# A Hymba decoder layer on one core: the mixer's weights split ahead and kept in DRAM, and work moved between the engines

## The chip, the cores and the metric

One Trainium2 chip, and of it one core. The metric is the device time of one execution in microseconds (us). TensorE is called PE here, VectorE DVE, ScalarE ACT, GpSimd POOL; SyncE (SP) issues all of the kernel's DMAs through one queue, in order.

## The reference

A decoder layer with three sub-layers on 512 tokens of width 1024, in fp32, each modulated from a vector `c` and followed by a layer norm:

```python
h = swiglu_ffn(modulate(x, sh1, sc1), w1, w3, w2)          # D_FF = 2816
x = layer_norm(alpha * x + 0.5 * g1 * h)
h = hybrid_mixer(modulate(x, sh2, sc2), ...)
x = layer_norm(alpha * x + g2 * h)
h = swiglu_ffn(modulate(x, sh3, sc3), ...)
x = layer_norm(alpha * x + 0.5 * g3 * h)

# hybrid_mixer: one input projection, then two groups
# A, 8 heads: indexer scores, the top 128 causal keys of each query, softmax attention over them
# B, 4 heads: short convolution, gated delta rule
proj  = u @ w_in
lower = beta * (k @ k.T) * dec_strict                      # delta rule, per chunk
w, u  = triangular_solve(lower + I, ...)                   # forward substitution
out   = qd @ S + aqk @ delta
dn    = rms_norm(dn, dn_norm_g) * silu(z)
return concat([attn_out, dn]) @ w_out
```

The modulation vectors (`mod`) are `silu(c)` times nine 1024x1024 matrices, 72 blocks of 128x1024 (`wada`).

## The kernel before

Every product of an activation with a weight is made of three matmuls in fp32r: both operands are split into a high part (a rounded copy) and a low part (the rest), and hi x hi, hi x lo and lo x hi are added in PSUM (`mm3`). For a weight block, a load puts 128x1024 into one of five buffers (`raw`), ACT copies 512 columns at a time to `wh`, and DVE or POOL subtracts to `wl` (`weights`; with `pool=True` some of the subtractions are POOL's).

The stages, by the span of the profile: the first gate columns of FFN1 with the first modulation vectors (0 to 62 us); FFN1's loop over 18 blocks of the hidden width (`f`, 48 matmuls of 512 columns each, to 258 us); FFN1's second product, eight output blocks (`dt`, 66 matmuls of 512 columns each) with the layer norm's sums (to 381 us); the norm and the mixer's first six column blocks (tile `g`, weights `wina`, to 421 us); the mixer proper (to about 680 us); its output product and the second norm (to 756 us); FFN2.

The mixer makes 20 projections (`project`, tile `pj`, weights `winb`, 24 matmuls of 512 columns each), the index scores (`ix`), the top-k by repeated maximum on DVE (`m`, `sc`), the softmax (`lg`, `x`; `nm` and `sum` are its row statistics), the values (`pt`, `pth`, `ptl`, `pv`), and the delta rule: `norms` and `pre` (decays `lam`, `er`; products `F`, `aq`), `sub` (forward substitution on 32x32 blocks, tiles `bl` and `Y`, 31 pairs of a multiplication and a subtraction on 64 partitions; its result goes through DRAM to get the layouts `X` and `XT`), `m` (blocks joined to 64 and 128), `rec` (recurrence over four chunks) and `out` (normalisation).

No operation is issued as written. `Graph.add` records all of them, a planner puts them in order by priorities that follow the order of the program, and one line (L561) emits them; rows are therefore read by their tiles. The order of the mixer's parts comes from the string `ORDER`: names with, after a colon, a delay of priority. Buffers are limited: five of `raw`, 86 of 128x512, eight PSUM banks. The modulation blocks (`ada`) are spread over FFN1: two per `f`, three per `dt`.

Of the kernel before, what the change touches and what calls it, by code (L numbers as in the profile page):

```python
# [11 lines left out]
F32 = mybir.dt.float32  # L12
# [15 lines left out]
SKEW, DEFER = 3, 500  # L28
ALPHA = 2.0 ** 0.25
# [535 lines left out]
class Build:  # L565
# [124 lines left out]

    def glu(s, p1, p3):
# [6 lines left out]
    def first_group(s, src, us, halves, big=False):  # L698


        nb = src.shape[2] // P
# [23 lines left out]
    def ffn(s, n, us, halves, ada_plan, res):  # L725
# [11 lines left out]
        for f in range(NF - G0[n]):  # L737
# [7 lines left out]
            s.ada_some(ada_plan(f))  # L745
        ws = {}
        for dt, c0, c1 in pieces(2):
# [11 lines left out]
            s.ada_some(ada_plan(100 + dt))  # L759
# [83 lines left out]
def body(s):  # L843
# [32 lines left out]
    s.ffn(1, us1, ALL, lambda f: 2 if f < 100 else 3, res1)  # L876
# [99 lines left out]
    s.ffn(2, u3, HALF, lambda f: 0, res3)  # L976
# [194 lines left out]
def attend_weights(s, q, k, bias, qt):  # L1171
    nc = s.nc
    w = (qt + 1) * P
    ps = []
    for h in range(4):
# [5 lines left out]
        mx, nm, sm = s.sm(1, "mx"), s.sm(1, "nm"), s.sm(1, "sum")  # L1181
        nc.vector.tensor_tensor_reduce(x[:, :w], pb[:, :w], bias[:, :w], 1.0, GONE, ALU.add, ALU.max, mx)
        nc.vector.tensor_scalar(nm, mx, -0.125, None, op0=ALU.mult)
        nc.scalar.activation(x[:, :w], x[:, :w], AF.Exp, bias=nm, scale=0.125, accum_out=sm)
        nc.vector.reciprocal(sm, sm)
        nc.gpsimd.tensor_scalar(x[:, :w], x[:, :w], sm, 1.0, op0=ALU.mult, op1=ALU.mult)
        ps.append(x)
    return ps


def attend_values(s, ps, v2, qt, g, att):
# [18 lines left out]
    for j in range(2):  # L1210
# [6 lines left out]
ORDER = ("first qi0 qa0:5766 ks:51 pk1:451 spill:57 pk3:1103 pq1:8 z2 qi1:17 gt:131 ix1 pv2:684 pq2:3860 pk2:1987 "  # L1217
# [22 lines left out]
class Mixer:  # L1240
# [59 lines left out]
    def gt(s):  # L1300
# [14 lines left out]
        nc.vector.tensor_copy(s.slr, b.c_("sl"))  # L1315
        cum = b.bank("cum")
# [84 lines left out]
    def pre(s, c):  # L1401
# [38 lines left out]
    def sub(s):  # L1440

        b, nc = s.b, s.nc
        B, n = 32, 64
        bl, Y = (b.g.tile(b.wraw, [P, B * B], F32, "raw", b.name(t), NRAW)[:n] for t in ("bl", "Y"))
        tmp = b.sc[:n]
# [4 lines left out]
        sq3 = lambda x: x.rearrange("p (a b) -> p a b", a=B)  # L1450
# [11 lines left out]
        nc.vector.tensor_copy(sq3(bl), y3.rearrange("p a b -> p b a"))  # L1462
        for src, lst, nme, eng in ((Y, s.X, "dX", nc.vector), (bl, s.XT, "dXT", nc.gpsimd)):
            d = b.g.tile(b.dram, [n, B * B], F32, nme, nme)
            nc.sync.dma_start(d, src)
            g = b.t("G").rearrange("p (u j) -> p u j", u=16)
            nc.sync.dma_start(g, d.rearrange("(u b) (i j) -> (b i) u j", u=16, i=B))
            for c in range(4):
                lst[c] = b.t("X")
                eng.tensor_mul(lst[c].rearrange("p (h b j) -> p h b j", h=4, b=4),  # L1470
                               g[:, 4 * c:4 * c + 4].unsqueeze(2).broadcast_to([P, 4, 4, B]),
                               b.c_("blk").unsqueeze(1).unsqueeze(3).broadcast_to([P, 4, 4, B]))

    def m(s, m, c):

        b, nc, hs, X, XT = s.b, s.nc, s.hs, s.X[c], s.XT[c]
        lm = b.t("lm")
        nc.gpsimd.tensor_mul(h4(lm), h4(s.F[c]), bc4(b.c_(f"m{m}")))
        p1 = b.bank("y1")
        for h in range(4):  # L1480
            nc.tensor.matmul(p1[:, hs[h]], lm[:, hs[h]], X[:, hs[h]], start=True, stop=True)
        y1 = b.t("y1")
        nc.scalar.activation(y1, p1, AF.Copy)
        p3 = b.bank("y3")
        for h in range(4):
            nc.tensor.matmul(p3[:, hs[h]], y1[:, hs[h]], XT[:, hs[h]], start=True, stop=True)
        if m < 128:
            p2 = b.bank("y2")
            for h in range(4):
                nc.tensor.matmul(p2[:, hs[h]], XT[:, hs[h]], y1[:, hs[h]], start=True, stop=True)  # L1490
            nc.vector.tensor_sub(X, X, p2)
        nc.vector.tensor_sub(XT, XT, p3)
# [46 lines left out]
    def out(s, c):  # L1539
# [74 lines left out]
```

## Time and profile before

| | us |
|---|---|
| median of 3 runs | 1100.04 (1100.03 to 1100.62) |
| profiled execution, its own time | 1099.98 |
| its span | 1098.2 |
| PE busy | 1061.3 |
| DVE busy | 679.3 |
| ACT busy | 414.9 |
| POOL busy | 302.3 |

The profiled execution is read by stages of the span: the table of windows gives, for each, how long every engine was busy, and the clock that PE was granted (1.00 is 2.4 GHz, 0.50 is 1.2 GHz). Some 1.8 us of the execution lie outside the span.

### The profile page before, as it was taken

To read this page: it belongs to the slowest core of one execution; us is meant where nothing else is said; L and a number is where in the kernel's file an instruction comes from. 1 tells how busy PE (TensorE), PEld (TensorE's weight loads), DVE (VectorE), ACT (ScalarE), POOL (GpSimd) and SP (SyncE) were. 2 spreads that over 40 slices of the span, in tenths; PEclk is the share of its full clock that TensorE was granted. 3 is DMA by queue.
4 is the path that set the end of the run, shared out by engine and by line. 5 is a ranking of instruction groups with operands and counts; after the bars stand their busy time and mean duration, and the time that the engine had idled before them with its cause. 6 is when DMAs were issued, how large, how long until landed. Compare 5 with 4: busy or idle time off the path is not lost.

```text
span 1098.2 us, 15160 instructions
## 1 busy us (share of the span) xinstructions
PE 1061.3 (97%) x5520; PEld 904.5 (82%) x5520; DVE 679.3 (62%) x1506; ACT 414.9 (38%) x866; POOL 302.3 (28%) x308
## 2 busy tenths in 40 slices
PE   8999999999999989999969999999999999999996
PEld 6788888888888988787747898989888888888896
DVE  7997655547672466999988999884333323333314
ACT  3353323233231434765832566443333322322203
POOL 4600000000222695496824311695000000002210
PEclk9999999999999999998959999999999999999998
DMA  9878555547642412131112303611323222243002
GB/s 359 314 278 316 206 179 196 172 138 244 221 156 91 137 54 98 40 109 46 44 43 52 103 21 125 235 45 41 113 83 110 92 81 72 68 144 106 16 1 77
DMA packets 52203, 137.92 MB, mean 126 GB/s; under 512 B 11360, under 2 KB 15584, under 8 KB 52128
## 3 DMA queue, kind: packets, MB, share of 16 engines
q1 hardware_dynamic: 52048, 136.69, 37.4%
q8 instruction: 43, 0.70, 0.3%
q14 instruction: 32, 0.26, 0.1%
q0 software_dynamic: 80, 0.26, 0.1%
HBM read 131.17 MB, written 5.77 MB: 125 GB/s over the span
## 4 chain that ended last, share of the span: by engine, by line
PE 75%; DVE 15%; issue 3%; ACT 3%; POOL 3%; DMA 1%; SPq 0%; POOLq 0%; ACTq 0%; DVEq 0%
PE p L561 37%; PE y L561 26%; PE g L561 6%; DVE sc L561 2%; DVE raw L561 2%; POOL wl L561 2%; DVE m L561 1%; PE pv L561 1%; DVE cv L561 1%; DVE x L561 1%; PE pj L561 1%; DVE u L561 1%; DVE Y L561 1%; PE pt L561 1%; DVE ptl L561 1%
## 5 line engine op out<-in xcount | busy, mean ns | idle before, releaser
L561 DVE TENSOR_TENSOR wl<-raw,wh 128x512 fp32r<-128x512 f32 (+1 forms) x260 | 180.1, 709 | 151.8 <-ACT wh L561 79.5
L561 ACT ACTIVATE wh<-raw 128x512 fp32r<-128x512 f32 (+1 forms) x300 | 174.7, 615 | 186.1 <-PE y L561 82.4
L561 PE MATMUL p<-ul,wh 128*128 128x512 f32 x592 | 230.3, 389 | 0.0
L561 PE MATMUL p<-uh,wh 128*128 128x512 f32 x592 | 230.3, 389 | 0.0
L561 PE MATMUL p<-uh,wl 128*128 128x512 f32 x592 | 230.3, 389 | 0.0
L561 PE MATMUL y<-hh,wl 128*128 128x512 f32 (+1 forms) x440 | 152.9, 347 | 0.0
L561 PE MATMUL y<-hl,wh 128*128 128x512 f32 (+1 forms) x440 | 152.7, 347 | 0.0
L561 PE MATMUL y<-hh,wh 128*128 128x512 f32 (+1 forms) x440 | 152.5, 347 | 0.0
L561 DVE CUSTOM_DVE_ANT_0 raw<-raw,silu_c 128x1024 f32<-128x1024 f32 x72 | 96.8, 1354 | 75.5 <-DMA raw<-in_wada_dram 75.5
L561 POOL TENSOR_SCALAR s<-x 128x512 f32<-128x512 f32 x3 | 4.0, 1332 | 461.4 <-DVE x L561 461.4
L561 PEld LDWEIGHTS p<-ul,wh 128*128 128x128 f32 x592 | 111.2, 188 | 23.2
L561 PEld LDWEIGHTS p<-uh,wl 128*128 128x128 f32 x592 | 111.1, 188 | 22.9
L561 PEld LDWEIGHTS p<-uh,wh 128*128 128x128 f32 x592 | 111.2, 188 | 22.8
L561 PEld LDWEIGHTS y<-hh,wh 128*128 128x128 f32 x440 | 83.3, 189 | 10.4
L561 PEld LDWEIGHTS y<-hl,wh 128*128 128x128 f32 x440 | 83.3, 189 | 10.4
L561 PEld LDWEIGHTS y<-hh,wl 128*128 128x128 f32 x440 | 83.3, 189 | 10.2
L561 ACT ACTIVATE hh<-sil 128x512 fp32r<-128x512 f32 x44 | 27.7, 633 | 154.9 <-DVE sil L561 135.0
L561 PE MATMUL g<-ul,wh 128*128 128x256 f32 (+1 forms) x256 | 78.8, 319 | 1.7 <-DVE ul L561 1.6
L561 PE MATMUL g<-uh,wh 128*128 128x256 f32 (+1 forms) x256 | 66.4, 316 | 9.9 <-ACT uh L561 9.9
L561 PE MATMUL g<-uh,wl 128*128 128x256 f32 (+1 forms) x256 | 75.5, 316 | 0.0
L561 POOL TENSOR_TENSOR wl<-wb,wh 128x512 fp32r<-128x512 f32 (+1 forms) x48 | 61.1, 1295 | 22.6 <-DMA wb<-in_f1a_dram 18.1
L561 POOL TENSOR_TENSOR s<-s,x 128x512 f32<-128x512 f32 (+1 forms) x21 | 28.5, 1356 | 137.0 <-DVE x L561 126.0
(254 smaller groups left out, 1826.8 us busy)
## 6 DMA issues: line engine op xcount, KB each, us to landing
raw<-in_wada_dram SPq DMA_DIRECT2D x72, 512.0 KB
raw<-in_f2b_dram SPq DMA_DIRECT2D x38, 512.0 KB
raw<-in_f1b_dram SPq DMA_DIRECT2D x36, 512.0 KB
raw<-in_winb_dram SPq DMA_DIRECT2D x20, 512.0 KB
raw<-in_f1c_dram SPq DMA_DIRECT2D x16, 512.0 KB
raw<-in_f2c_dram SPq DMA_DIRECT2D x16, 512.0 KB
wb<-in_f1a_dram SPq DMA_DIRECT2D x16, 256.0 KB
raw<-in_wout_dram SPq DMA_DIRECT2D x8, 512.0 KB
```

Of the source, the lines that this page charges most:

```text
L561: getattr(getattr(s.nc, o.eng), o.meth)(*[real(x) for x in o.args], **{k: real(v) for k, v in o.kw.items()})
```

## The change

1. `presplit`, called in FFN1 once per `f` and twice per `dt`, takes a weight block of the mixer (8 of `wina`, 128x768; 20 of `winb`, 128x1024), loads it to `raw`, splits it (ACT copies to a second `raw` buffer, DVE subtracts in place) and writes both halves to DRAM. In the mixer `stored` loads hi and lo; nothing is split there any more for these 28 blocks.
2. The `ada` blocks are three per `dt` only for the first four `dt`; the last eight move to FFN2.
3. `sub` runs on 128 partitions: the even columns of `Y` on the lower 64, the odd on the upper. One transposed copy (`YT`) goes through DRAM instead of two; `X` is made by transposes on PE and an ACT copy.
4. `m`: the parts that are known to be zero are left out; no mask product on POOL for 128.
5. Softmax: `nm` and `sum` are made for four heads in one instruction; the final scaling of `x` goes from POOL to ACT.
6. `pre`: the decay products `lam` and the scaling of `er` go from POOL to ACT, in pieces of one head; the mask becomes one more matmul.
7. `norms`: squares from POOL to ACT. `out`: the Newton steps of `rsqrt` on DVE become one power on POOL; the scaling of `o` goes from DVE to ACT.
8. `ORDER` is another string.

```diff
+PRE_F, PRE_D = 1, 2
+    def presplit(s):
+        nc = s.nc
+        if s.pre_next >= KD + 20:
+            return
+        i, s.pre_next = s.pre_next, s.pre_next + 1
+        n, src = (768, s.d["wina"][i]) if i < KD else (1024, s.d["winb"][i - KD])
+        dst = s.dwa[i] if i < KD else s.dwb[i - KD]
+        raw = s.wload(src, n)
+        hi = s.g.tile(s.wraw, [P, 1024], F32, "raw", s.name("rawh"), NRAW)
+        nc.scalar.activation(hi[:, :n].bitcast(F32R), raw[:, :n], AF.Copy)
+        nc.vector.tensor_sub(raw[:, :n].bitcast(F32R), raw[:, :n], hi[:, :n])
+        nc.sync.dma_start(dst[0], hi[:, :n])
+        nc.sync.dma_start(dst[1], raw[:, :n])
+    def stored(s, src, n, big=False):
...
+                x = s.g.tile(s.wraw, [P, 1024], F32, "raw", s.name("wd"), NRAW)
+                nc.sync.dma_start(x[:, :n], src[j])
...
+    def plan(s, f):
+        s.ada_some(2 if f < 100 else 3 if f < 104 else 0)
+        for _ in range(PRE_F if f < 100 else PRE_D):
+            s.presplit()
...
-        w = s.weights(s.d["winb"][i + b], 1024, pool=True)
+        w = s.stored(s.dwb[i + b], 1024)
...
-        nc.vector.tensor_scalar(nm, mx, -0.125, None, op0=ALU.mult)
-        nc.scalar.activation(x[:, :w], x[:, :w], AF.Exp, bias=nm, scale=0.125, accum_out=sm)
-        nc.vector.reciprocal(sm, sm)
-        nc.gpsimd.tensor_scalar(x[:, :w], x[:, :w], sm, 1.0, op0=ALU.mult, op1=ALU.mult)
+    nc.vector.tensor_scalar(nm, mx, -0.125, None, op0=ALU.mult)
+    for h, x in enumerate(ps):
+        nc.scalar.activation(x[:, :w], x[:, :w], AF.Exp, bias=nm[:, h:h + 1], scale=0.125, accum_out=sm[:, h:h + 1])
+    nc.vector.reciprocal(sm, sm)
+    for h, x in enumerate(ps):
+        nc.scalar.activation(x[:, :w], x[:, :w], AF.Identity, scale=sm[:, h:h + 1])
...
-            nc.gpsimd.tensor_mul(h4(lam), bc4(b.c_("triu")),
-                                 part[:, 4 * c:4 * c + 4].unsqueeze(2).broadcast_to([P, 4, P]))
-            nc.tensor.matmul(eb, s.slr, lam, start=j == 0, stop=j == 1)
+            for h in range(4):
+                i = c * 4 + h
+                nc.scalar.activation(lam[:, hs[h]], b.c_("triu"), AF.Identity, scale=part[:, i:i + 1])
+            nc.tensor.matmul(eb, s.slr, lam, start=j == 0, stop=False)
+        nc.tensor.matmul(h4(eb), s.idr, bc4(s.below), start=False, stop=True)
...
-            t3 = tmp[:, 0:r * (j + 1)].rearrange("p (a b) -> p a b", a=r)
-            nc.vector.tensor_mul(t3, b3[:, j, j + 1:B].unsqueeze(2).broadcast_to([n, r, j + 1]),
-                                 y3[:, j, 0:j + 1].unsqueeze(1).broadcast_to([n, r, j + 1]))
-            nc.vector.tensor_sub(y3[:, j + 1:B, 0:j + 1], y3[:, j + 1:B, 0:j + 1], t3)
+            r, m = B - 1 - j, j // 2 + 1
+            t3 = tmp[:, 0:r * m].rearrange("p (a b) -> p a b", a=r)
+            nc.vector.tensor_mul(t3, b3[:, j, j + 1:B].unsqueeze(2).broadcast_to([P, r, m]),
+                                 y3[:, j, 0:m].unsqueeze(1).broadcast_to([P, r, m]))
+            nc.vector.tensor_sub(y3[:, j + 1:B, 0:m], y3[:, j + 1:B, 0:m], t3)
...
+            px = b.bank("X")
+            for h in range(4):
+                nc.tensor.transpose(px[:, hs[h]], XT[:, hs[h]], b.c_("ident"))
+            X = s.X[c] = b.t("X")
+            nc.scalar.activation(X, px, AF.Copy)
...
-        cf = b.rsqrt(v, 4)
+        cf = b.sm(4, "cf")
+        nc.gpsimd.tensor_tensor(cf, v, b.c_("mhalf").broadcast_to([P, 4]), op=ALU.pow)
         nc.vector.tensor_mul(cf, cf, rq4)
         for h in range(4):
-            nc.vector.tensor_scalar(o[:, hs[h]], o[:, hs[h]], cf[:, h:h + 1], None, op0=ALU.mult)
+            nc.scalar.activation(o[:, hs[h]], o[:, hs[h]], AF.Identity, scale=cf[:, h:h + 1])
```

Three places of the order that comes out of it. The first is SP's queue in FFN1's loop. Before, one `f` issues four loads, two of weights for FFN1 (`in_f1b`) and two of modulation blocks:

```order
L561 DMA raw_777<-in_f1b_dram 128x1024
L561 DMA raw_796<-in_f1b_dram 128x1024
L561 DMA raw_807<-in_wada_dram 128x1024
L561 DMA raw_815<-in_wada_dram 128x1024
L561 DMA raw_826<-in_f1b_dram 128x1024
```

Now one `f` issues seven:

```order
L562 DMA raw_1079<-in_wina_dram 128x768
L562 DMA raw_1087<-in_f1b_dram 128x1024
L562 DMA raw_1103<-in_f1b_dram 128x1024
L562 DMA raw_1107<-in_wada_dram 128x1024
L562 DMA dwa<-rawh_1101 128x768
L562 DMA dwa<-raw_1079 128x768
L562 DMA raw_1143<-in_wada_dram 128x1024
```

What moved: a load of a mixer block stands ahead of FFN1's own, and two writes, which need ACT's and DVE's halves, stand ahead of the second modulation block. Six `raw` buffers are taken per `f` where four were.

The second is DVE at the start of `sub` (`tmp` or `silu_c` takes the product). Before, on 64 partitions, among it the low parts `ptl` of the attention values:

```order
L561 RECIPROCAL sum_5313<-sum_5313 128x1
L561 RECIPROCAL sum_5318<-sum_5318 128x1
L561 TENSOR_TENSOR silu_c<-bl_5075,Y_5277 64x31
L561 TENSOR_TENSOR Y_5277<-Y_5277,silu_c 64x31
L561 TENSOR_TENSOR silu_c<-bl_5075,Y_5277 64x60
L561 TENSOR_TENSOR Y_5277<-Y_5277,silu_c 64x30x2
L561 TENSOR_TENSOR silu_c<-bl_5075,Y_5277 64x87
L561 TENSOR_TENSOR ptl_5336<-pt_5320,pth_5331 128x512
L561 TENSOR_TENSOR Y_5277<-Y_5277,silu_c 64x29x3
```

Now, on 128 partitions, among the last of the top-k:

```order
L562 TENSOR_TENSOR tmp_5355<-bl_5111,Y_4932 128x31
L562 MAX m_932_5357<-sc_4395 128x8
L562 TENSOR_TENSOR Y_4932<-Y_4932,tmp_5355 128x31
L562 MATCH_REPLACE sc_4395<-m_932_5357,sc_4395 128x256
L562 TENSOR_TENSOR tmp_5355<-bl_5111,Y_4932 128x30
L562 TENSOR_SCALAR sc_4395<-sc_4395 128x256
L562 TENSOR_TENSOR Y_4932<-Y_4932,tmp_5355 128x30
L562 TENSOR_TENSOR tmp_5355<-bl_5111,Y_4932 128x58
L562 TENSOR_TENSOR Y_4932<-Y_4932,tmp_5355 128x29x2
```

What moved: the substitution stands beside the last rounds of the top-k instead of beside the attention's values, and its second and third pairs are half as wide.

The third is ACT's queue where the softmax and the values of several heads stand. Before, exponentials (`x,sum<-x,nm`) are followed at once by the high parts `pth` of the transposed weights:

```order
L561 ACTIVATE x_5267,sum_5289<-x_5267,nm_5281 128x384
L561 ACTIVATE x_5270,sum_5299<-x_5270,nm_5293 128x384
L561 ACTIVATE x_5284,sum_5313<-x_5284,nm_5305 128x384
L561 ACTIVATE x_5295,sum_5318<-x_5295,nm_5308 128x384
L561 ACTIVATE pth_5331<-pt_5320 128x512
L561 ACTIVATE pth_5355<-pt_5341 128x512
```

Now the scalings (`x<-x,sum`), the copies of `X` and the exponentials of the next heads stand in one queue:

```order
L562 ACTIVATE x_5716,sum_5763<-x_5716,nm_5731 128x384
L562 ACTIVATE th_5844<-pj_5586 128x512
L562 ACTIVATE x_5722,sum_5852<-x_5722,nm_5773 128x512
L562 ACTIVATE x_5733,sum_5852<-x_5733,nm_5773 128x512
L562 ACTIVATE X_5872<-X_5861 128x512
L562 ACTIVATE ath_5416<-pv_5837 128x128
L562 ACTIVATE ath_5425<-pv_5837 128x128
L562 ACTIVATE x_5688<-x_5688,sum_5763 128x384
L562 ACTIVATE X_5891<-X_5876 128x512
```

What moved: a scaling that POOL made beside ACT now waits its turn behind ACT's other work, and the copy that the delta rule needs stands between exponentials.

## Rows read from the trace of the kernel before

**Rows 1.** Busy time of each engine by stage, PE's granted clock, DMA share, GB/s.
```profile
62.00:258.00 196.00, 196.00 (x867) 162.34 (x866) 125.66 (x239) 63.44 (x116) 0.00 (x0) 1.00 0.61 207
258.00:381.00 123.00, 123.00 (x676) 107.63 (x675) 65.40 (x134) 33.76 (x63) 34.92 (x31) 1.00 0.51 165
381.00:421.00 40.00, 37.13 (x297) 36.74 (x297) 20.66 (x40) 11.49 (x27) 38.85 (x48) 0.96 0.29 104
421.00:500.00 79.00, 77.36 (x350) 62.96 (x349) 74.14 (x172) 54.47 (x119) 47.89 (x40) 0.98 0.21 69
500.00:540.00 40.00, 37.98 (x192) 31.11 (x191) 38.31 (x101) 26.94 (x66) 28.69 (x29) 0.91 0.17 56
540.00:580.00 40.00, 29.78 (x125) 21.29 (x125) 35.37 (x131) 17.77 (x49) 18.10 (x30) 0.70 0.10 30
580.00:620.00 40.00, 38.88 (x216) 32.63 (x215) 34.57 (x64) 11.80 (x22) 13.22 (x11) 1.00 0.33 93
620.00:680.00 60.00, 59.67 (x455) 55.23 (x454) 55.92 (x247) 39.16 (x127) 9.66 (x16) 1.00 0.17 58
```

**Rows 2.** Groups of PE's waits, 381 to 740 us: total us, times, longest.
```profile
PE pv L561 <- ACT pth L561: 4.0, 5, 1.3
PE pt L561 <- POOL x L561: 1.1, 3, 0.7
```

**Rows 3.** PE in order of time, one wait of the attention: start, us, idle before.
```profile
561.48 0.58 PE L561 MATMUL pv<-pth,vh 128*128 128x256 f32 x1 [0.69 <-ACT pth L561]
```

**Rows 4.** Groups of DVE's instructions, 421 to 710 us: busy, mean ns, idle before.
```profile
L561 DVE TENSOR_TENSOR wl<-raw,wh 128x512 fp32r<-128x512 f32 x31 | 28.0, 926 | 4.4 <-ACT wh L561 4.4
...
L561 DVE TENSOR_TENSOR qs<-rp,qs 64x512 fp32r<-64x512 f32 x16 | 14.5, 904 | 0.4
...
L561 DVE TENSOR_TENSOR Y<-Y,silu_c 64x31 f32<-64x31 f32 (+15 forms) x31 | 12.6, 407 | 0.9
L561 DVE TENSOR_TENSOR silu_c<-bl,Y 64x31 f32<-64x31 f32 (+15 forms) x31 | 11.6, 375 | 1.1 <-POOL x L561 0.2
L561 DVE TENSOR_TENSOR X<-X,y 128x512 f32<-128x512 f32 x12 | 7.9, 683 | 1.3 <-PE y L561 1.2
...
L561 DVE RECIPROCAL sum<-sum 128x1 f32<-128x1 f32 x32 | 4.9, 156 | 1.4 <-ACT x L561 1.3
...
L561 DVE TENSOR_SCALAR nm<-mx 128x1 f32<-128x1 f32 x32 | 4.4, 143 | 0.0
...
L561 DVE TENSOR_SCALAR o<-o,rs 128x128 f32<-128x128 f32 x16 | 3.8, 282 | 0.0
...
L561 DVE TENSOR_TENSOR rs<-rs,rs 128x4 f32<-128x4 f32 (+1 forms) x15 | 3.3, 234 | 0.1
```

**Rows 5.** Groups of POOL's instructions, 381 to 710 us.
```profile
L561 POOL TENSOR_TENSOR wl<-raw,wh 128x512 fp32r<-128x512 f32 x36 | 48.4, 1360 | 28.7 <-ACT wh L561 20.8 <-PE pj L561 7.9
L561 POOL TENSOR_SCALAR x<-x,sum 128x256 f32<-128x256 f32 (+3 forms) x32 | 19.1, 605 | 61.7 <-DVE nm L561 30.7 <-PE pt L561 14.9 <-DVE sum L561 10.9
```

**Rows 6.** Groups of ACT's instructions, 381 to 710 us.
```profile
L561 ACT ACTIVATE wh<-raw 128x512 fp32r<-128x512 f32 x65 | 38.5, 628 | 24.3 <-DMA raw<-in_wout_dram 15.7 <-DMA raw<-in_f2b_dram 6.8 <-PE pj L561 1.7
L561 ACT ACTIVATE x<-x,nm 128x256 f32<-128x256 f32 (+3 forms) x32 | 17.7, 556 | 15.6 <-DVE nm L561 13.9 <-issue 1.6
...
L561 ACT ACTIVATE ktok<-ktok,nm 128x128 f32<-128x128 f32 x16 | 5.0, 412 | 0.0
```

**Rows 7.** Groups of DVE's instructions in FFN1's loop, 62 to 258 us.
```profile
L561 DVE TENSOR_TENSOR wl<-raw,wh 128x512 fp32r<-128x512 f32 x79 | 52.4, 680 | 11.5 <-PE p L561 9.9 <-ACT wh L561 1.3
L561 DVE CUSTOM_DVE_ANT_0 raw<-raw,silu_c 128x1024 f32<-128x1024 f32 x40 | 48.6, 1224 | 51.4 <-DMA raw<-in_wada_dram 51.4
```

**Rows 8.** Busy time in the window with the most DMA traffic, columns as in the first group.
```profile
20.00:40.00 20.00, 17.62 (x68) 13.71 (x69) 19.93 (x27) 6.96 (x12) 14.53 (x9) 0.91 1.04 399
```

**Rows 9.** The chain that ended last: a load of 512 KB, start, us.
```profile
598.38 4.51 DMA raw<-in_wout_dram
```

More of the change, by code (lines that the diff above doesn't have):

```diff
@@ L643, in weights, with get @@
         return get
+    def presplit(s):
[12 more added lines that the diff above has]
+    def stored(s, src, n, big=False):
+        nc = s.nc
+        parts = []
+        for j in range(2):
+            if big:
+                ts = []
+                for o in range(0, n, 512):
+                    m = min(512, n - o)
+                    q, s.g.quota = s.g.quota, s.quota
+                    x = s.t("wd")[:, :m]
+                    s.g.quota = q
+                    s.g.late = s.g.ahead
+                    nc.sync.dma_start(x, src[j][:, o:o + m])
+                    s.g.late = 0
+                    ts.append(x)
+                parts.append(ts)
+            else:
+                x = s.g.tile(s.wraw, [P, 1024], F32, "raw", s.name("wd"), NRAW)
+                nc.sync.dma_start(x[:, :n], src[j])
+                parts.append([x[:, o:o + 512] for o in range(0, n, 512)])
+        def get(i):
+            o = (i % 4) * P
+            return tuple(ts[i // 4][:, o:o + P].bitcast(F32R) for ts in parts)
+        return get
     def mm3(s, out, wh, wl, xh, xl, start, stop):
@@ L744, in ffn @@
             hs.append(s.glu(p1, p3))
-            s.ada_some(ada_plan(f))
+            ada_plan(f)
         ws = {}
@@ L758, in ffn @@
                 del ws[dt]
[L759 removed]
+            ada_plan(100 + dt)
     def rsqrt(s, v, w, n=3):
@@ L1174, in attend_weights @@
     ps = []
+    mx, nm, sm = s.sm(4, "mx"), s.sm(4, "nm"), s.sm(4, "sum")
     for h in range(4):
@@ L1315, in gt @@
         nc.vector.tensor_copy(s.slr, b.c_("sl"))
+        s.idr, s.below = b.keep(P, "idr", F32R), b.keep(P, "below", F32R)
+        nc.vector.tensor_copy(s.idr, b.c_("ident"))
+        nc.vector.tensor_scalar(s.below, b.c_("sl"), NEG, None, op0=ALU.mult)
         cum = b.bank("cum")
@@ L1440, in sub @@
     def sub(s):
[L1442 to L1445, printed above, removed]
+        b, nc, hs = s.b, s.nc, s.hs
+        B, n, w = 32, 64, 16
+        bl = b.g.tile(b.wraw, [P, B * B], F32, "raw", b.name("bl"), NRAW)
+        Y, YT, tmp = b.t("Y"), b.t("YT"), b.t("tmp")
         for c in range(4):
@@ L1462, in sub @@
[L1462 to L1472, printed above, removed]
@@ new lines, in sub @@
+        nc.vector.tensor_copy(YT.rearrange("p (a b) -> p a b", a=w), y3.rearrange("p a b -> p b a"))
+        d = b.g.tile(b.dram, [n, B * B], F32, "dXT", "dXT")
+        halves = d.rearrange("b (m q) -> b m q", m=w)
+        for odd in range(2):
+            nc.sync.dma_start(halves[:, :, odd * B:odd * B + B],
+                              YT[odd * n:odd * n + n].rearrange("p (a b) -> p a b", a=w))
+        g = b.t("G").rearrange("p (u j) -> p u j", u=16)
+        nc.sync.dma_start(g, d.rearrange("(u b) (i j) -> (b i) u j", u=16, i=B))
@@ new lines, in sub @@
+        for c in range(4):
+            XT = s.XT[c] = b.t("XT")
+            nc.vector.tensor_mul(XT.rearrange("p (h b j) -> p h b j", h=4, b=4),
+                                 g[:, 4 * c:4 * c + 4].unsqueeze(2).broadcast_to([P, 4, 4, B]),
+                                 b.c_("blk").unsqueeze(1).unsqueeze(3).broadcast_to([P, 4, 4, B]))
+    def m(s, m, c):
+        b, nc, hs, XT = s.b, s.nc, s.hs, s.XT[c]
+        if m == 64:
+            px = b.bank("X")
[3 more added lines that the diff above has]
+            nc.scalar.activation(X, px, AF.Copy)
+            lm = b.t("lm")
+            nc.gpsimd.tensor_mul(h4(lm), h4(s.F[c]), bc4(b.c_("m64")))
+            p1, p2, p3 = b.bank("y1"), b.bank("y2"), b.bank("y3")
+            for h in range(4):
+                nc.tensor.matmul(p1[:, hs[h]], lm[:, hs[h]], X[:, hs[h]], start=True, stop=True)
+            y1 = b.t("y1")
+            nc.scalar.activation(y1, p1, AF.Copy)
+            for h in range(4):
+                nc.tensor.matmul(p3[:, hs[h]], y1[:, hs[h]], XT[:, hs[h]], start=True, stop=True)
+            for h in range(4):
+                nc.tensor.matmul(p2[:, 32 * h:32 * h + 32], XT[:, hs[h]], y1[:, h * P:h * P + 32], start=True, stop=True)
+            x = h4(X)[:, :, 0:32]
+            nc.vector.tensor_sub(x, x, p2[:, 0:P].rearrange("p (h j) -> p h j", h=4))
+            x, y = (v.rearrange("p (u j) -> p u j", u=8)[:, :, 32:64] for v in (XT, p3))
+            nc.vector.tensor_sub(x, x, y)
+            return
+        X, F, a, e = s.X[c], s.F[c], slice(0, 64), slice(64, 128)
+        p1, p3 = b.bank("y1"), b.bank("y3")
@@ L1487, in m @@
[L1487 to L1492, printed above, removed]
+            nc.tensor.matmul(p3[a, 64 * h:64 * h + 64], y1[e, 64 * h:64 * h + 64], XT[e, h * P + 64:h * P + P],
+                             start=True, stop=True)
+        x = h4(XT)[a, :, 64:128]
+        nc.vector.tensor_sub(x, x, p3[a, 0:256].rearrange("p (h j) -> p h j", h=4))
```

47 lines of the change are left out of this document (22 added, 25 removed), and 10 rows, old and new, of the table ORDER.

## The prediction

> **What bounds the kernel now.** I read the table of stages first [rows 1]. In FFN1 the matmul engine is busy all the time at full clock: 867 matmuls in 196.00 us are 0.226 us each, and nothing but fewer or later matmuls could change these stages. From 381 to 680 us it is not. There I add, stage by stage, what PE stands idle (2.9, 1.6, 2.0, 10.2, 1.1, 0.3: 18.2 us) and what it loses to the lower clock, which is the missing share of the clock times the stretch (0.04 x 40, 0.02 x 79, 0.09 x 40, 0.30 x 40: 18.8 us). Together that is 37 us, an upper bound for the loss, since some of the low clock falls on idle time. The stretch from 500 to 580 us has 27.8 of the 37. Second, in the same table, who is full there: DVE is busy 73.7 of those 80 us, and 238.3 of the 259 us from 421 to 680, while PE's work in these 259 us, without idle time and at full clock, would be 259 - 15.3 - 17.2 = 226.5 us. So DVE has more to do than PE in the mixer. Third, the waits: the groups that end PE's idle time are ACT's `pth` and POOL's scaled `x` [rows 2], short links of the attention's chain [rows 3]. I read the two together so: DVE sets the pace of the stretch, and where its queue is late, PE waits on whatever link it feeds.
>
> **What the change takes from DVE in the mixer** [rows 4]. (a) `sub`: 62 instructions of mean 391 ns. A one-column instruction takes 143 to 156 ns, so some 150 is fixed and 240 goes with width; half the columns give 270 ns: 62 x 0.12 = 7.5 us. (b) Row statistics: 64 instructions become 16, of the same 0.15 us: 7.2 us. (c) The scaling of `o`: 3.8 us. (d) Newton steps: four calls of about a dozen narrow instructions, 0.14 to 0.23 us each, 7 to 11 us; I take 8. (e) `m`: 12 subtractions of 683 ns become four each of 128, 256 and 256 columns, some 0.28 and twice 0.42 us by interpolation: 3.5 us. (f) DVE's instructions are longer while POOL works: `wl` takes 926 ns here and 680 in FFN1's loop [rows 4, 7], where POOL does nothing [rows 1]; `qs` takes 904 where `X`, as wide, takes 683. These two groups alone are 7.6 + 3.5 = 11 us, and POOL gives up its largest groups [rows 5]. Sum 41 us: 238 becomes 197, under PE's 226. The new copies (one `YT` for one `bl`, four `XT` for four `X`) cancel.
>
> **What it adds to ACT there** [rows 6]. Out: 40 splits of `winb`, 25 us. In: 32 scalings of `x`, which are as wide as the exponentials (0.556 us): 17.8; 32 `lam`, 16 `er` and 16 `o` pieces of 128 columns with a scale from a column, as `ktok` has (0.412 us): 26.4; squares and copies of `X`, eight of about 0.6: 5. ACT had 150 us in 421 to 680 [rows 1]; it gets 174 of about 229. It remains below PE; the cover is the slack of 55 us, and it is thinnest after `sub`, which is the second rival's place. The row statistics now wait for four heads together, so a first head starts later by up to three DVE instructions; I leave that in what is not recovered.
>
> Here a rule speaks against the change. `ktok` on ACT takes 412 ns, `o` on DVE, as wide, 282 [rows 4, 6]: a multiplication is 0.13 us cheaper on DVE. The Trainium skill ("ScalarE: Activation LUTs", Rules for kernel authors) says that multiplications belong on VectorE and not on ScalarE; the rows agree in direction. By the rule the 64 narrow pieces waste 64 x 0.13 = 8.3 us, and the time would be 1088 rather than 1080 if all of it lay on the path. By the rows only the 16 `o` come from DVE, and DVE is the full engine, so I charge nothing.
>
> **What it adds to FFN1.** 28 blocks are read and written twice over. Compute: in the loop, 18 subtractions on DVE of up to twice 0.68 us are at most 24.5 us beside 125.7 of 196 busy, and 18 copies on ACT about 23 us beside 63.4 [rows 1, 7]; PE covers both. Traffic: the loop moves 207 GB/s x 196 us = 40.6 MB and gets 25.1 MB more, 335 GB/s. That is under the 399 GB/s that the startup reaches [rows 8]. The first four `dt` each move 1.44 MB of own weights, three modulation blocks (1.57 MB) and two presplit blocks (3.15 MB): 6.16 MB, 15.4 us at 399 GB/s against 66 x 0.226 = 14.9 us. That is 0.5 us each, 2 us in all, as a middle: nothing if the weights split ahead cover it, 9 us if the rate is a tenth lower.
>
> Buffers: a loop pass takes six of the five `raw` slots in 10.85 us, so a slot may be held 9.0 us on average. By the rows a load takes 4.5 us from issue to landing [rows 9], two high parts 1.26 [rows 6], two low parts 1.36 or a modulation product 1.22 [rows 7]; a write, which no row shows, I take like the load. That gives 7.1 for a weight slot, 5.7 for a modulation slot, 11.6 for the presplit's first buffer and 5.8 for its second: mean 7.2 us. In the first four `dt` it is 7.3 us against 7.5 allowed. It just fits, so I charge nothing for it here. In the mixer a projection holds two of the five slots for 24 x 0.226 = 5.4 us, and its successor's two loads and the first of the next fit in the other three: no charge.
>
> **PE's own work.** 16 transposes of 128 columns between 0.06 and 0.23 us each (a quarter and the whole of a 512-column matmul) and four mask matmuls of 0.23 come in; narrower matmuls in `m` go out, at most about what the transposes cost. Bounds -1 to +4.5; I take 2.5, nearer the upper end, since the transposes are of fp32 and their rows could be dearer than a quarter.
>
> **The sum.** PE recovers 25 of the 37 us: nine tenths of the 27.8 between 500 and 580, where DVE is full; the remaining 9 us I leave, since part of it is the norm's chain ahead of 421 us, which stays. 25 - 2.5 - 2 = 20.5 us. The profiled execution took 1099.98 us, 1.8 over its span and equal to the median of the runs (1100.04) to within 0.1 us, so the forecast is 1080. Its own range: all 37 recovered and the other terms at their good ends give 1064; half recovered (18) with 4.5 and 3 against it, 1090.
>
> **Rivals.**
> *ACT becomes the bound behind `sub`.* From 620 to 680 us ACT is busy 39.2 of 60 us already [rows 1]; half of the 32 scalings (9), all `o` (6.6) and the copies of `X` (2.4) would make it 57 to 60 us, with the waits of a queue in order on top. If the stretch keeps its length rather than giving way to other work, about 10 us of the gain go: 1090. For it: the scaled `x` and the copy of `X` stand between exponentials. Against it: the new order can take exponentials earlier, into 540 to 620, where ACT was busy 29.6 of 80 us. Chance 0.17. (The Trainium skill's rule on multiplications, "ScalarE: Activation LUTs", Rules for kernel authors, would be paid for here.)
>
> *The attention's chain stays the wait.* The change doesn't do what it seems to: PE waits 0.7 us a time for `pth` [rows 3], a chain of PE, ACT, DVE and PE that is as long as ever, and the link from POOL only changes engine. If the holes around 560 us are such latencies, the low clock stays too, and a few of the 28 us return: 4 + 2 - 2.5 - 2, between 1096 and 1100. Against it: these named waits are only 5.1 us in all [rows 2] beside 18 of idle time. Chance 0.11.
>
> *FFN1 starves (the other side).* Mechanism: a `raw` slot is held longer than reckoned, because SP issues in order and a write that waits for DVE's half keeps the next loads behind it. A pass of the loop then lasts 6/5 of the hold, a `dt` twice the hold. At 2 us more (9.2 and 9.3) this is 18 x 0.2 + 4 x 3.7 = 18 us; at 2.5 us more 18 x 0.8 + 4 x 4.7 = 33 us, and the time is about 1111. It decides from some 2.2 us on, where the gain of 22.5 is gone. For it: the fit is 7.3 of 7.5. Against it: what is split ahead lies between, and the loop has 1.8 us of room. A milder form is the rate: the Trainium skill ("DMA: Bandwidth & Descriptors", Specifications) gives a core about 358 GB/s of HBM; by it a `dt` would last 17.2 us, 9 us in all, and the time be 1087. The startup's 399 GB/s [rows 8] contradict it for reads; no row has writes in such number. Chance that the end is above before: 0.12.
>
> **The numbers.** Forecast 0.60, ACT-bound 0.17, chain stays 0.11, FFN1 starves 0.12. Predicted 1080. The range reaches from 1065 to 1098: it holds nearly all of the first, the second and most of the third, some 0.83. A measurement of this kernel can tell 0.2% (2.2 us) from no change: faster 0.83 (the first two and half of the third), same 0.04, slower 0.13.
>
> **What would show it.** Right: in FFN1 PE stays at 100% and clock 1.00, DMA near 335 GB/s in the loop; in the stretch of the mixer PE's clock is 1.00 nearly throughout, DVE's busy share falls below 90%, the two instructions of `sub` take about 270 ns, `wl` returns to about 680. ACT-bound: the waits of PE after `sub` are all for ACT and ACT is over 95% busy for 40 us. Chain: the low clock is where `pv` waits for `pth`. Starved: PE waits for `wl` or `wh` between 62 and 345 us, and SP's queue waits for `rawh` or the presplit's subtraction.

## The result and the profile after

The changed kernel takes 1085.49 us (median of four runs, 1082.78 to 1086.81) against 1100.03: a ratio of 0.9865 with an interval of 0.9844 to 0.9886. It is faster by 14.5 us, clear of the scatter of both, where 20 were forecast. The profiled execution took 1084.83 us with a span of 1083.1.

The stages after, in the same windows as [rows 1] (busy time of PE, weight loads, DVE, ACT, POOL; PE's clock; DMA share; GB/s):

```profile
62.00:258.00 196.00, 196.00 (x866) 162.38 (x865) 139.22 (x243) 79.97 (x131) 0.00 (x0) 1.00 0.91 324
258.00:381.00 123.00, 117.10 (x602) 100.52 (x602) 72.69 (x124) 37.38 (x63) 21.21 (x19) 0.97 0.78 280
381.00:421.00 40.00, 38.63 (x323) 38.43 (x323) 21.73 (x49) 9.00 (x20) 25.23 (x35) 1.00 0.46 152
421.00:500.00 79.00, 78.10 (x377) 62.91 (x377) 65.33 (x148) 49.49 (x120) 10.06 (x8) 1.00 0.33 119
500.00:540.00 40.00, 39.26 (x210) 32.65 (x209) 39.91 (x115) 28.77 (x74) 8.96 (x11) 1.00 0.37 123
540.00:580.00 40.00, 39.53 (x215) 32.88 (x214) 38.02 (x131) 20.66 (x57) 2.59 (x2) 1.00 0.46 157
580.00:620.00 40.00, 37.90 (x275) 33.57 (x274) 30.45 (x110) 37.23 (x110) 1.02 (x1) 1.00 0.30 86
620.00:680.00 60.00, 60.00 (x402) 53.95 (x401) 52.84 (x130) 42.75 (x115) 14.39 (x10) 1.00 0.42 138
```

From 421 to 680 us PE now has the full clock throughout and 4.2 us of idle time, where it had 15.3 and a clock of 0.70 at worst. But from 258 to 381 us, where it never waited, it has 5.9 us of idle time and a clock of 0.97, and it does 602 matmuls there instead of 676. A new loss stands where there was none.

Windows of equal time hold different work in the two kernels. The next table therefore goes by events: the starts of the first and last matmuls of a stage in each trace (all times in us).

| stage | before | after | change |
|---|---|---|---|
| FFN1's last product | at 380.9 | at 389.7 | +8.8 |
| the mixer's first column blocks (`g`) | 41.0 | 37.9 | -3.1 |
| from there to the last product of `wout` | 292.7 | 269.7 | -23.0 |
| from there to the last `g` of FFN2 | 40.8 | 43.4 | +2.6 |
| rest of FFN2 | 330.3 | 330.0 | -0.3 |

The sum is -15.0 us. What ended PE's longest waits after the change, from 52 to 756 us (total, times, longest):

```profile
PE y L562 <- ACT wh L562: 5.9, 1, 5.9
PE st L562 <- DVE s L562: 2.2, 2, 1.4
PE g L562 <- ACT uh L562: 1.9, 3, 1.4
PE pv L562 <- DVE ptl L562: 1.0, 2, 0.7
...
PE pv L562 <- DVE sum L562: 0.4, 1, 0.4
...
PE pt L562 <- ACT x L562: 0.3, 1, 0.3
```

The attention's waits of [rows 2], 5.1 us, are down to 1.7. The longest wait is now one of 5.9 us for a weight of FFN1. The chain of what ended last, in order of time (start, us), tells how it came about:

```profile
295.43 1.07 ACT rawh L562
296.50 0.02 issue
296.53 1.24 DVE raw L562
297.78 0.44 SPq L562
298.22 0.04 issue
298.29 0.03 issue
298.31 6.22 DMA raw<-in_f1c_dram
...
317.88 1.22 DVE raw L562
319.09 0.02 DVE mod L562
319.13 3.62 DMA raw<-in_f1c_dram
...
322.83 0.64 ACT wh L562
323.47 0.04 issue
323.51 50.01 PE y L562 x275
```

A presplit block is split; only then SP's queue goes on to the load of FFN1's own weights, which takes 6.2 us to land. A second time the load stands until DVE has finished with a modulation block (`mod`) at 319.1, since no slot was free. Between the two, DVE was busy with the rotary tables (`cos`, `sin`). What SP's queue itself waited for from 250 to 345 us (total, times, longest):

```profile
SPq L562 <- ACT rawh L562: 23.4, 6, 6.1
...
SPq L562 <- DVE mod L562: 10.7, 5, 4.5
```

The loss of 8.8 us is more than the wait. PE in order of time (start, us), and the window behind the wait:

```profile
323.51 0.80 PE L562 MATMUL y<-hh,wh 128*128 128x512 f32 x1 [5.90 <-ACT wh L562]
324.10 0.63 PE L562 MATMUL y<-hl,wh 128*128 128x512 f32 x1
324.53 0.63 PE L562 MATMUL y<-hh,wl 128*128 128x512 f32 x1
```
```profile
322.00:332.00 10.00, 8.49 (x26) 6.73 (x27) 5.10 (x8) 5.03 (x9) 3.52 (x3) 0.66 0.83 302
```

The granted clock, 1.00 up to the wait, is at its lower level behind it (0.50 from 323.6 to 328 us): the starts of the next thirteen matmuls are 0.59 us (once) and 0.43 us apart, where they were 0.227 apart before. So 6.1 us of the 8.8 are PE standing and 2.8 are the lower clock.

In the mixer, the engines from the last of its first blocks to the first product of `wout`, before (first row) and after (second):

```profile
422.00:664.40 242.40, 227.13 (x1241) 190.00 (x1239) 222.09 (x632) 141.10 (x352) 115.42 (x119) 0.93 0.20 62
```
```profile
427.60:647.30 219.70, 215.50 (x1253) 181.84 (x1253) 194.52 (x566) 156.89 (x418) 23.89 (x23) 1.00 0.35 119
```

The stage is 22.7 us shorter. PE stands idle in it for 4.2 us instead of 15.3, and it is busy for 215.5 us instead of 227.1 with about as many matmuls (1253 and 1241), while the granted clock is 1.00 instead of 0.93: about half of the gain is idle time, the other half is clock. For this stage DVE has 27.6 us less to do, POOL 91.5 less and ACT 15.8 more. The groups on DVE that answer to [rows 4] (428 to 698 us; busy, mean ns):

```profile
L562 DVE TENSOR_TENSOR wl<-raw,wh 128x512 fp32r<-128x512 f32 x32 | 29.7, 954 | 0.6 <-ACT wh L562 0.5
...
L562 DVE TENSOR_TENSOR qs<-rp,qs 64x512 fp32r<-64x512 f32 x16 | 11.0, 686 | 1.3 <-ACT qs L562 0.9
L562 DVE TENSOR_TENSOR Y<-Y,tmp 128x126 f32<-128x126 f32 (+22 forms) x31 | 7.9, 254 | 0.6
L562 DVE TENSOR_TENSOR tmp<-bl,Y 128x126 f32<-128x126 f32 (+22 forms) x31 | 7.8, 253 | 1.0 <-issue 0.4
...
L562 DVE RECIPROCAL sum<-sum 128x4 f32<-128x4 f32 x8 | 1.4, 172 | 2.6 <-ACT x L562 2.6
L562 DVE TENSOR_SCALAR nm<-mx 128x4 f32<-128x4 f32 x8 | 1.3, 162 | 0.0
```

`sub`'s two groups are 15.7 us instead of 24.2, `qs` is back to 686 ns, and `wl` is not: 954 ns.

### The profile page after: what moved, and what is told of

Same layout as the page of the kernel before. It is cut to its first block, busy times and chain, and to the rows that moved or that the text cites. A ratio compares the mean times of both kernels' runs of the same rounds, so it can differ in the third digit from the quotient of the medians.

```text
span 1083.1 us, 15160 instructions
## 1 busy us (share of the span) xinstructions
PE 1052.2 (97%) x5540; PEld 898.4 (83%) x5540; DVE 677.2 (63%) x1424; ACT 448.5 (41%) x941; POOL 186.9 (17%) x185
## 4 chain that ended last, share of the span: by engine, by line
PE 75%; DVE 12%; DMA 5%; ACT 3%; issue 3%; POOL 1%; SPq 1%; POOLq 0%; ACTq 0%; DVEq 0%
PE p L562 37%; PE y L562 23%; PE g L562 5%; PE pj L562 4%; DVE raw L562 3%; DVE sc L562 2%; DMA raw<-in_f1c_dram 2%; DVE m L562 1%; PE pv L562 1%; DMA raw<-in_winb_dram 1%; DVE x L562 1%; DVE cv L562 1%; DVE u L562 1%; DMA wd<-dwb 1%; ACT rl L562 1%
## 5 line engine op out<-in xcount | busy, mean ns | idle before, releaser
L562 ACT ACTIVATE wh<-raw 128x512 fp32r<-128x512 f32 (+1 forms) x260 | 149.1, 611 | 131.1 <-PE y L562 48.3
L562 DVE CUSTOM_DVE_ANT_0 raw<-raw,silu_c 128x1024 f32<-128x1024 f32 x72 | 100.3, 1399 | 40.0 <-DMA raw<-in_wada_dram 39.8
L562 PE MATMUL pj<-uh,wd 128*128 128x512 f32 x320 | 104.6, 399 | 0.5 <-DMA wd<-dwb 0.4
L562 ACT ACTIVATE rawh<-raw 128x1024 fp32r<-128x1024 f32 (+1 forms) x28 | 28.0, 1000 | 107.2 <-DMA raw<-in_winb_dram 73.6
L562 PEld LDWEIGHTS pj<-uh,wd 128*128 128x128 f32 x320 | 59.4, 188 | 13.8 <-DMA wd<-dwb 1.5
L562 PE MATMUL pj<-ul,wd 128*128 128x512 f32 x160 | 62.3, 395 | 0.0
L562 ACT ACTIVATE hh<-sil 128x512 fp32r<-128x512 f32 x44 | 27.6, 631 | 83.4 <-DVE sil L562 70.9
```

Source lines behind the costliest of these rows:

```text
L562: getattr(getattr(s.nc, o.eng), o.meth)(*[real(x) for x in o.args], **{k: real(v) for k, v in o.kw.items()})
```

## The experiments

Stage times below are read from the profiled execution, by the first and last matmuls as in the table above; "the mixer" is its third row. In three of the kernels the line that emits all operations is L563.

**Why FFN1 is late: slots or bytes.** One more slot:

```diff
-NBIG, NRAW, WF, WM, WB, W2 = 86, 5, 32, 16, 28, 28
+NBIG, NRAW, WF, WM, WB, W2 = 84, 6, 32, 10, 28, 28
```

> The changed kernel with six raw slots instead of five (paid for with two of the 86 small buffers and a smaller quota of split weights in the mixer, so the mixer may lose a little). It asks why FFN1 ends 8.8 us later than before (389.7 instead of 380.9 us). Theory S, slots and order: SP's in-order queue waits for a slot that DVE frees late, and the next loads wait behind it; a sixth slot lets them start, and FFN1 ends at 381 to 385 us. Theory R, rate: the first four output blocks want 411 GB/s, which the DMA engines don't give; a sixth slot brings no bytes, and FFN1 ends at 388 to 390 us.

FFN1 ended at 380.8 us. The window of its second half:

```profile
258.00:381.00 123.00, 123.00 (x676) 107.61 (x675) 70.57 (x128) 37.61 (x63) 29.29 (x29) 1.00 0.74 263
```

All 676 matmuls are back and the loss of 8.8 us is gone, with every byte still moved. So it was slots, and not the rate. SP's queue still waits 22.0 us for `rawh` between 250 and 345 us, where it was 23.4; with one more slot this no longer reaches PE. The whole took 1087.67 us (0.9893, 0.9878 to 0.9908), since the mixer, with two small buffers fewer and a smaller quota of split weights, takes 277.8 us and the second norm's stage 50.1.

Fewer bytes written:

```diff
-        nc.sync.dma_start(dst[0], hi[:, :n])
-        nc.sync.dma_start(dst[1], raw[:, :n])
+        nc.sync.dma_start(dst[0][:, :P], hi[:, :P])
+        nc.sync.dma_start(dst[1][:, :P], raw[:, :P])
...
```

> The changed kernel with each presplit write cut to its first 128 columns, which the mixer's loads then read over and over (so its weights are others): 24 of the 27 MB written in FFN1 are gone, while slots, splits and the queue's order stay. Theory R (rate): the loss in FFN1 is gone, it ends at 381 to 382 us. Theory S (slots and order): each slot is freed a little earlier by a shorter write, the waits for DVE stay, and half of the loss or more stays: FFN1 ends at 385 to 389 us. The mixer's time isn't read from it.

FFN1 ended at 381.6 us, sooner than theory S allowed and where theory R had it. This run alone would have spoken for the rate, which the run before it rules out at the full traffic. What fits both is how long a slot is held: SP's waits for a write to land (`dwb`) fall from 14.3 us to 8.9 between 250 and 345 us, and those for `rawh` from 23.4 to 12.6. That shorter holding alone did it here wasn't tried apart from the bytes. (The whole was 1096.9 us; its mixer loads in pieces of 128 columns and isn't compared.)

Presplit spread out:

```diff
-        s.ada_some(2 if f < 100 else 3 if f < 104 else 0)
-        for _ in range(PRE_F if f < 100 else PRE_D):
+        s.ada_some(2 if f < 106 else 0)
+        for _ in range(2 if f < 2 else 1):
             s.presplit()
```

> The changed kernel with the presplit spread: one block per output block over all eight (and two in the first two passes of the loop), and two modulation blocks per output block over six instead of three over four. The traffic per output block falls from 6.2 to 4.1 MB, the slots taken from ten to seven. Both theories on FFN1 expect its end at 381 to 384 us and the whole at 1077 to 1081. If neither is right and FFN1 is late by DVE's own work alone (the rotary tables stand in the same place), it ends at 386 to 390 and the whole stays at 1083 to 1086.

FFN1 ended at 380.8 us and the whole took 1077.32 (0.9800, 0.9784 to 0.9816), 8.2 us under the changed kernel. So the rotary tables on DVE, which are still made there, don't make FFN1 late by themselves.

Besides, the last modulation blocks later:

```diff
-    s.ffn(2, u3, HALF, lambda f: s.ada_some(1), res3)
+    s.ffn(2, u3, HALF, lambda f: s.ada_some(1 if 8 <= f < 100 else 0), res3)
```

> The spread presplit of the earlier run, and the last eight modulation blocks put into FFN2's later passes (from the eighth on) instead of its first, so that their products don't stand on DVE within the second norm. From the last product of wout to the end of FFN2's first column blocks it lasts 43.4 us in the changed kernel and 40.8 before. If these products are the cause, it returns to 40 to 41.5 us and the whole is 1074 to 1076; if the norm is late by another cause (waits for POOL's low parts), it stays at 43 and the whole at 1077.

The second norm's stage took 39.6 us (42.7 in the spread kernel), and its waits for `s` on DVE are gone:

```profile
PE g L562 <- DVE ul L562: 0.9, 3, 0.3
PE g L562 <- ACT uh L562: 0.7, 1, 0.7
```

The whole took 1075.55 us (0.9781, 0.9766 to 0.9795). This is the fastest version, 9.9 us under the changed kernel; its lead of 1.8 over the spread one is within their scatter (1074.83 to 1077.94 and 1076.30 to 1079.29), while the stage's 3.1 us is read in the trace.

**Whether the parts gain by themselves.** Weights alone (the mixer's operations and order as before; `sub` with a scratch tile of its own):

> Only the weights' part of the change: presplit, stored weights and the new places of the modulation blocks, with the mixer's operations and its order as before. Main theory (DVE sets the mixer's pace, and most of the relief is from sub, softmax, out and m, less from POOL's splits): FFN1 loses its 9 us, the mixer gains 8 to 14, the whole is 1094 to 1102. Rival (the splits on POOL and ACT were what held the mixer): the mixer gains over 20, the whole is 1084 to 1089.

It took 1134.97 us (1.0323, 1.0307 to 1.0338), outside both expectations: the mixer needs 316 us. PE's waits there are new ones:

```profile
PE y L562 <- POOL X L562: 7.6, 1, 7.6
...
PE pj L562 <- DMA wd<-dwb: 6.8, 5, 3.4
PE y L562 <- DVE X L562: 3.9, 4, 1.4
```

The projections wait for stored weights and the delta rule for `X`. By the code the old `sub` keeps two of the five slots and a stored projection two more; that this is the cause wasn't tried apart.

The order alone undone (`ORDER` of before in the changed kernel):

> The changed kernel with the ORDER string of before, all else changed. The mixer from its first column blocks to the last product of wout lasts 292.7 us before, 269.7 in the changed kernel and 315.9 with the presplit alone under the old order. Theory O (the operations carry the gain: less on DVE, one raw slot less held by sub): 272 to 284 us, the whole 1087 to 1099. Theory P (stored weights need the new order, since each projection holds two of five raw slots): over 295 us, the whole over 1108.

It took 1141.05 us (1.0372, 1.0353 to 1.0392), the mixer 324.1: theory P by its number, but the main wait is not for weights:

```profile
PE X L562 <- DVE XT L562: 19.9, 1, 19.9
```

The presplit undone, the new order kept:

```diff
-PRE_F, PRE_D = 1, 2
+PRE_F, PRE_D = 0, 0
...
-        w = s.stored(s.dwb[i + b], 1024)
+        w = s.weights(s.d["winb"][i + b], 1024, pool=True)
...
```

> The changed kernel without the presplit: the mixer splits its weights as before on ACT and POOL, with the new operations and the new order (the quota of split weights in the mixer is 12 instead of 16, or no order exists). FFN1 must end at 380 to 382 us instead of 389.7. Theory D (the mixer's gain comes from DVE's operations): first blocks 41 us as before, the mixer 268 to 276 us, the whole 1076 to 1083, better than the changed kernel. Theory W (the splits on POOL and ACT slow the mixer): 282 us and more, the whole over 1089.

FFN1 ended at 380.9 us as expected, but the whole took 1150.21 (1.0452, 1.0434 to 1.0469) and the mixer 337.0, with the same wait grown:

```profile
PE X L562 <- DVE XT L562: 31.7, 1, 31.7
```

The new operations without presplit, in the old order:

> The new operations without the presplit, in the order of before (the quota of split weights in the mixer is 12 instead of 16, or no order exists). With the kernel before, the presplit alone and the operations with presplit, it makes the square at the old order. FFN1 ends at 380 to 382 us. Theory D (the operations relieve DVE and gain by themselves): the mixer 270 to 285 us against 292.7 before, the whole 1078 to 1093. Theory P (only parts, weights and order together gain): 293 to 330 us, the whole over 1100.

It took 1151.2 us (1.0474, 1.0447 to 1.0500), the mixer 336.9, and the longest wait is again for `XT`:

```profile
PE X L562 <- DVE XT L562: 13.1, 1, 13.1
```

So at the old order each part loses, 35 us and 51, and the two together 41; at the new order the whole change gains 14.5, and without the presplit it loses 50. My theory that the operations relieve DVE and so gain by themselves falls. What these four have in common is seen in the waits: where the result of `sub` comes back from DRAM, PE stands, in three of them for `XT` and in the first 7.6 us for `X`. In the changed kernel 82 of the projections' 480 recorded matmuls run beside `sub`, and logits and values of the attention beside the trip; without the presplit, under the same order, none runs beside `sub` and 72 follow it. These runs don't price a part: none of the four has an order made for it, and two have a smaller quota of split weights.

**Whether ACT became the bound.** Four kinds of scaling given back (`x`, `lam`, `er` to POOL, `o` to DVE; the planner orders anew):

> The changed kernel with the scalings of x, lam and er back on POOL and that of o back on DVE, in the new order. If ACT had become the bound behind sub (the first rival), the mixer falls from 269.7 to 260 to 266 us, the whole to 1075 to 1081. If not (forecast), the mixer is as long or longer, since POOL's long instructions are back in the chain of the attention and beside DVE: 270 to 282 us, the whole 1085 to 1097.

It took 1104.29 us (1.0044, 1.0027 to 1.0061), the mixer 286.9. The sign is against the first rival, but the planner has made another order: the `XT` products of the last two chunks come at 626.8 and 629.5 us instead of 599.3 and 600.3.

Therefore the scaling of `x` alone, with the order of every engine frozen: the planner orders the changed kernel, and the instruction is replaced when it is emitted.

```diff
...
+    if o.meth == "activation" and name(0)[:2] == "x_" and "scale" in o.kw and isinstance(o.kw["scale"], View) \
+            and o.kw["scale"].tile.name[:3] == "sum":
+        return [("gpsimd", "tensor_scalar", (o.args[0], o.args[1], o.kw["scale"], 1.0),
+                 dict(op0=ALU.mult, op1=ALU.mult))]
```

> The changed kernel with every instruction in its place on its engine, except that the 32 scalings of x go from ACT to POOL at the point of the order where they stand. So no planner decides anew, as it did where four kinds of work were given back. From the last of the mixer's first column blocks to the last product of wout the changed kernel takes 269.7 us. ACT as the bound behind sub (first rival): 260 to 266 us, since ACT is rid of about 18 us. Forecast's view (ACT has cover): 268 to 274 us, POOL's instructions a little longer in the chain and beside DVE.

It took 1085.11 us (0.9866, 0.9845 to 0.9886), the mixer 271.1, beside 1085.49 and 269.7. ACT is rid of a group of 16.1 us, and nothing is gained, though the scaling takes hardly longer on POOL (598 ns, 556 on ACT) and DVE is no busier for it (194.6 us in the stage, 194.5 in the changed kernel): ACT was not the bound.

**Whether DVE still is.** Both in the frozen order. `sub`'s products twice:

```diff
...
+    if o.meth == "tensor_mul" and name(0)[:3] == "tmp":
+        return [(o.eng, o.meth, o.args, o.kw)] * 2
```

> The changed kernel with the same order, and each of the 31 multiplications of sub issued twice (the second writes the same values): some 7.8 us more of DVE's time, about what the halving of sub's width was reckoned to give. If DVE still sets the pace around sub, or sub's chain is on the path, the mixer is longer by 5 to 9 us: 275 to 279. If both are covered by the projections that stand beside it, 269 to 272 us.

The group `tmp` doubled to 15.7 us (7.9 more), `sub` lasted 35.4 us instead of 26.5, and the mixer 282.5 in the profiled execution, 12.8 more. That is more than either expectation. The whole took 1095.21 (0.9949, 0.9925 to 0.9974; 1087.99 to 1098.55, the profiled one being the longest), 9.7 more by the medians. PE waits for a scaled `x` whose reciprocal stood behind `sub`'s work on DVE, and for a rotary product (`rq`) that stood there too:

```profile
PE pt L563 <- ACT x L563: 4.5, 2, 4.3
...
PE sw L563 <- DVE rq L563: 1.8, 1, 1.8
```

The row statistics by head:

```diff
...
+    if (o.meth == "tensor_scalar" and name(1)[:2] == "mx") or (o.meth == "reciprocal" and name(0)[:3] == "sum"):
+        cut = lambda x, h: x[:, h:h + 1] if isinstance(x, View) else x
+        return [(o.eng, o.meth, tuple(cut(x, h) for x in o.args), o.kw) for h in range(4)]
```

> The changed kernel with the same order, and the 16 instructions for the row statistics of four heads issued as 64 for one head, at the same places: some 7 us more of DVE's time, spread over the attention. If DVE's time is worth its length in the mixer: 274 to 278 us. If DVE is no longer the bound: 269 to 272 us.

It took 1086.21 us (0.9870, 0.9854 to 0.9886), the mixer 271.7. But the two groups on DVE (428 to 700 us) did not grow by 7 us:

```profile
L563 DVE RECIPROCAL sum<-sum 128x1 f32<-128x1 f32 x32 | 3.0, 148 | 2.0 <-ACT x L563 2.0
L563 DVE TENSOR_SCALAR nm<-mx 128x1 f32<-128x1 f32 x32 | 2.6, 143 | 0.0
```

They were busy 2.7 us and are now busy 5.6: four instructions of 148 ns in a row overlap. Some 2.9 us more on DVE, then, came with 2.0 us more in the mixer and 0.7 by the medians, both within the scatter of the runs (1083.10 to 1087.19). This run can't tell a price of nothing from one of a microsecond for a microsecond. In `sub`, where DVE is nearly full (25.6 of the 27 us from 559 to 586), a microsecond of DVE's cost about one; what it costs elsewhere stays open.

## Why the prediction was right, and where it was not

The range (1065 to 1098) and the direction held; the likeliest time was 5.5 us too low. (The best case of the sum, put at 1064, is 1062 by its own terms, 1100 - 37 - 1.)

*What bounds the kernel.* Right as to the place: of the 37 us of idle time and low clock that I read from [rows 1] between 381 and 680 us, the same stretch now shows 5.6 and full clock. By stages, the first blocks and the mixer are 26.1 us shorter; with PE's added work that is a recovery of 27, where I took 25. The reason that I gave, DVE having more to do than PE, is not borne out where it matters. My sign, a busy share of DVE under 90%, holds over the whole mixer (226.5 of the 259 us from 421 to 680), but not from 500 to 580 us, where most of the loss lay: there DVE is busy 77.9 of 80 us, more than before (73.7), and yet PE stands only 1.2 us and has full clock. That the 25 came so near is therefore in part luck. The reading of the waits was too narrow as well: of 14.2 us that PE waited between 421 and 680 us, `pth` and `x` ended 5.1 and DVE's own results 7.6.

*PE's own work.* I took 2.5 us. From start to start of the matmuls it is +1.0: transposes 1.7 (0.109 us each), mask matmuls 0.9, and `m` 1.7 less.

*DVE.* (a) `sub` was reckoned at 270 ns an instruction and takes 254; it gives 8.5 us for 7.5. (b) The row statistics give 6.6 for 7.2. (f) was half wrong: `qs` returned to 686 ns as forecast, `wl` did not. What [rows 4] counts there are not the mixer's splits: in both kernels they start at 592 to 594 us, for `wout` and FFN2, and 17 of the 31 of before stand behind 680 us. That POOL's work lengthens them is right: with POOL busy for over half of their time they take 1150 ns before and 1261 after, beside an idle POOL 688 and 683. But the second norm's sums on POOL (`s`, 22 us from 428 to 698 us) remain. DVE's work in the mixer fell by 27.6 us, not 41, and that sufficed. So the sum over DVE was the wrong measure. That 7.9 us in `sub` cost about 10 shows that DVE's work has its price where it is full and other results stand in its queue; for the rest of DVE's work no run shows a price.

*ACT.* Forecast: 24 us more, covered. Measured: 15.8 us more and no gain from taking 16 of them away. The first rival falls, though ACT came near: it is busy 37.2 of 40 us from 580 to 620, but from 580 to 680 PE waits only 2.1 us, 0.3 of them for ACT. The rule of the Trainium skill ("ScalarE: Activation LUTs", Rules for kernel authors) has its difference here too, `o` takes 402 ns on ACT and took 282 on DVE, but no price in the time could be shown for moving `x` off ACT; `o` by itself wasn't tried.

*The second rival,* that the attention's chain stays, falls too: its waits are 1.7 us where they were 5.1, and the clock from 540 to 580 us is 1.00.

*FFN1.* Here a step failed: I charged 2 us for traffic and nothing for slots. It cost 8.8, and the cause is the slots, as the third rival had it, in a milder form and with the signs that it named (PE waits for `wh`, SP's queue for `rawh`): with a sixth slot the cost is zero at the same traffic. The reckoning of 7.3 us of holding against 7.5 allowed took 4.5 us for a transfer; of the loads on the chain from 270 to 323 us three took 6.2 to 7.1 us, one 4.6 and the last 3.6, and DVE, which I took as always ready, had the rotary tables to make. Nor did I count that a wait is followed by a lower clock, here 2.8 us. That the rate's form of the rival gave 9 us too is coincidence. The rate of about 358 GB/s that the Trainium skill gives a core ("DMA: Bandwidth & Descriptors", Specifications) did not decide it: the window from 282 to 292 us moved 395 GB/s, reads and writes together.

```profile
282.00:292.00 10.00, 10.00 (x46) 8.29 (x45) 5.47 (x11) 2.61 (x5) 2.00 (x3) 1.00 1.03 395
```

*A cost I left out.* The eight moved modulation blocks stand on DVE within the second norm: +2.6 us, which go when they are put later.

So 27 recovered, 1.0 of added work, 8.8 and 2.6 lost, and 0.3 gained in FFN2: 15.0. The size was missed by FFN1's 6.8 and the norm's 2.6, against some 4 us better in the mixer. What the prediction took for granted, that the order would cover the chain, was the condition of the whole: under the order of before, the same operations and presplit lose 41 us.

What stays open is how the gain divides between the presplit and the operations: each needs an order of its own, and none was made.

## What to carry to other kernels

A transfer put into a busy stage was charged here by the buffers that it held, not by its bytes: count takings per pass, multiply by a holding time that is measured under load, and leave room for the engine that frees them. A wait of PE can cost more than its length, so look at the granted clock behind it. Where an order is made by a planner, undoing a part also makes another order; freeze the order and change the single instruction before reading a price. An engine's total busy time says who is full, not what a microsecond of its work costs. And before a run is read as a price, see in its trace that the work was added: 64 short instructions for 16 made 2.9 us, not 7.

## What the hardware showed unexpectedly

Fewer moving columns in `m`'s fp32 matmuls gave nothing; one group with fewer stationary columns was shorter. These groups of the changed kernel (590 to 660 us) name the rows and columns of the stationary operand (64*128), then its rows again with the moving columns (64x64); behind the bar stand busy time and mean ns:

```profile
L562 PE MATMUL y<-X,F 64*128 64x64 f32 x32 | 4.4, 278 | 0.0
L562 PE MATMUL y<-X,lm 128*128 128x128 f32 x32 | 4.3, 278 | 0.0
L562 PE MATMUL y<-y,XT 128*128 128x32 f32 x32 | 4.2, 264 | 0.0
...
L562 PE MATMUL y<-XT,y 64*64 64x64 f32 x32 | 2.6, 224 | 0.0
```

The first three have 64, 128 and 32 moving columns, and the median distance from one start to the next is 0.112 us in each. The last has 64 moving columns as the first, but 64 stationary ones instead of 128, and its distance is 0.058 us. Where `m` became 1.7 us cheaper, it is these 32 matmuls.

And the changed kernel's time scatters more than before: 1082.78 to 1086.81 us against 1099.13 to 1100.62.
